# A two-layer encoder trunk: interleaved Strassen products, an earlier copy of the bias table, a gain moved from weights to x, and joined key and value weights

## The chip, the cores and the metric

The kernel runs on one core of a Trainium2 chip. The metric is the device time of one execution in microseconds (us). Five engines work beside each other: TensorE (PE, matrix products), VectorE (DVE), ScalarE (ACT), GpSimd (POOL) and SyncE (SP, which issues most of the DMAs). Each engine takes its instructions in the order in which the program lists them.

## The reference

Two layers work on x of 512 frames by 1024 features. Layer 0 is a gated linear recurrence with a squared-ReLU MLP, layer 1 a differential attention with another squared-ReLU MLP. Keys and values of layer 1 come from the stream after layer 0. All in fp32:

```python
h = h + rms_norm(hgrn2_mixer(rms_norm(h, a_norm_pre), a_w_in, ...), a_norm_post)
h = h + rms_norm(squared_relu_mlp(rms_norm(h, mlp_norm_pre[0]), w_up[0], w_down[0]), ...)
k, v = split(rms_norm(h, kv_norm) @ w_kv)          # 1024 x 2048
q = rms_norm(h, b_norm_pre) @ b_w_q                # 8 heads, two maps each
p = softmax(q k^T / 8 + rel_bias, block-causal); attn = p[0] - lam * p[1]
h = h + rms_norm(rms_norm(attn @ v, subln) * c @ b_w_out, b_norm_post)
h = h + rms_norm(squared_relu_mlp(..., w_up[1], w_down[1]), ...)   # relu(h W)^2 W'
```

## The kernel before

**Products.** Every fp32 operand of a large product is held as a pair: a rounded high part and the rest (`xhi`/`xlo`, `whi`/`wlo`, `uhi`/`ulo`), and a product is three matmuls on the fast fp32r type (`mm3`). Features lie on partitions, frames on the free axis. A weight tile of 128x1024 fp32 comes by a DMA of SP into one of four `raw` buffers; ACT writes the high part (`whi`), DVE the rest (`wlo`), each into a ring of eight tiles (`split_w`, L161 to 179). Where the norm's gain belongs to the weight's rows, a tile is split in pieces, one for each 128 rows, with the gain as scale (L175, L176); without a gain the whole tile goes in one instruction (L167, L168).

**Order.** The program is made by generators under a planner (`Plan`), which counts matmul time and puts the waits of the chains at due times (`yield 10.0` means "10 us of matmul time later"). It fixes PE's order. The other engines are ordered by a scheduler that follows the dependences; a chain's instructions get a higher priority than the main line's.

**Stages.** `first_loads` brings in x and the weights of head 0; `start` computes the first norm's factor, spreads it over the partitions as `dg` (L628), and a matmul `ps_sp` (L631) turns that into the row `rb`. `hgrn` runs the eight heads. Then come the output product, the MLP (`block`), the boundary with keys, queries and values of the first two heads (`attention_first`), `attention`, its output product, and the second MLP.

**MLP.** The hidden 4096 features are four quarters. Quarter 0 is a plain product (`up`). Quarters 1 to 3 use Strassen's seven products: a quarter has four pairs (of two column blocks), and a pair (`up_pair`, L452) makes seven products `prod` of 12 matmuls of 128x256, into three banks `ux`, `uy`, `uz`. The order in a pair is a11 (`ux`), s1 (`uz`), s2 (`ux`), a12 (`uy`), s3 (`ux`), s4 (`uz`), a22 (`ux`). `ux` goes on summing while ACT copies it out between: `p1` behind the first product, `u2` behind s2 (L486), `p5` from `uz`. After the last product ACT applies ReLU, square and split (L501 to 504, L409, L410). The next pair starts behind the last product. Each quarter ends with a down product (`dn`). I call the 28 products of a quarter a group: three groups in each layer.

**Bias table.** `params` spawns at 60 us of the MLP and waits `yield 40.0` (L648), makes a table `bw` of 16x640 on PE and DVE (L656 to 661), and POOL copies it 32 times over into `bias_dr` in DRAM (L662), which `attend` reads later.

**Attention.** In each group of two heads keys, queries and values come from three weights (`w_k`, `w_q`, `w_v`), in the order k, q, k, q, v; the values' weight is loaded after the other two. Units of 128 queries (`unit`) make logits, softmax, transposes `pt`, copies `at` on ACT (L902) and products `ao`.

Of the kernel before, what the change touches and what calls it, by code (L numbers as in the profile page):

```python
# [88 lines left out]
def trunk_kernel(ctx: ExitStack, tc: tile.TileContext, x_t, w_qf, w_g, w_i, w_ao, w_k, w_q, w_v, w_bo, w_up, w_us, w_dn,  # L89
# [301 lines left out]
    def block(pool, proj, gpost, name, layer, want):  # L391
# [60 lines left out]
        def up_pair(q, p, ts):  # L452

            nm = f"{layer}_{q}_{p}"
            def raw(n):
                return wp.tile([P, 2, 512], F32, tag="raw", name=f"raw_{n}{nm}", bufs=4)

            ws = w_us[layer, q - 1]
            ra = raw("a")
            nc.sync.dma_start(ra, ws[p, :, 0:3:2, :])  # L460

            rs = raw("s")
            for i in range(2):
                nc.sync.dma_start(rs[:, i, :], ws[p, :, 3, :])
            g.dma_start(rs, ws[p, :, 0:2, :], accum_op=ALU.add)  # L465
            if p % 2 == 0:
                rd = raw("d")
                nc.sync.dma_start(rd, ws[p:p + 2, :, 1, :].rearrange("a p f -> p a f"))
                a22s[:] = split_b(rd, f"d{nm}")
            a11, a12 = split_b(ra, f"a{nm}")  # L470
            a22 = a22s[p % 2]
            s3, s1 = split_b(rs, f"s{nm}")
            v.tensor_tensor(ra[:, 0, :], ra[:, 0, :], rs[:, 1, :], op=ALU.add)
            v.tensor_tensor(ra[:, 1, :], ra[:, 1, :], ra[:, 0, :], op=ALU.add)
            s2, s4 = split_b(ra, f"t{nm}")
            px, py, pz = mmt(f"ux{nm}")[:, 0:256], smt(f"uy{nm}")[:, 0:256], smt(f"uz{nm}")[:, 0:256]
            r = pool.tile([P, 2, S], F32, tag="r", name=f"r{nm}", bufs=2)

            def prod(ps, w, b, first):
# [9 lines left out]
            yield from prod(px, a11, xpart(0, 0), True)
            p1 = keep(px, "p1")  # L490
            yield from prod(pz, s1, ts[0], True)
            p5 = keep(pz, "p5")
            yield from prod(px, s2, ts[2], False)
            u2 = keep(px, "u2")
            yield from prod(py, a12, xpart(1, 0), True)
            v.tensor_tensor(r[:, 0, 0:256], py, p1, op=ALU.add)
            yield from prod(px, s3, ts[1], False)
            v.tensor_tensor(r[:, 1, 256:512], px, p5, op=ALU.add)
            yield from prod(pz, s4, xpart(1, 1), False)
            v.tensor_tensor(r[:, 0, 256:512], pz, u2, op=ALU.add)  # L500
            a.activation(r[:, 0, :], r[:, 0, :], AF.Relu)  # L501
            a.activation(r[:, 1, 256:512], r[:, 1, 256:512], AF.Relu, scale=-1.0)
            yield from prod(px, a22, ts[3], False)
            a.activation(r[:, 1, 0:256], px, AF.Relu, scale=-1.0)
            keep_u(r, p, 0, S)

        for q in range(4):
            if q == 0:
                wt = [load_w(w_up[layer, i], 512, None, f"up{layer}_{i}") for i in range(2)]
                for h, (lo, hi) in enumerate(halves):  # L510
                    yield until(("x", name, h))
                    for pr in range(4):
                        ps = mmt(f"up{layer}_{h}_{pr}").rearrange("p (j t) -> p j t", j=2)
                        for j in range(2):
                            n = 2 * pr + j
                            for kt in range(8):
                                wmm(ps[:, j, :], wt[n // 4], kt, (n % 4) * P, xhi, xlo, lo, hi, kt == 0, kt == 7)
                                yield 0
                        split_u(ps, pr, lo, hi, f"r{layer}_{h}_{pr}")
                ts = sums_x()  # L520
            else:
                for p in range(4):
                    yield from up_pair(q, p, ts)
# [52 lines left out]
    def first_loads(hp):  # L576
# [22 lines left out]
        for pr in range(4):  # L599
            for j in range(2) if pr == 0 else (slice(0, 2),):  # L600
                a.activation(xhi[pr][:, j], raws[pr][:, j], AF.Copy)  # L601
                v.tensor_tensor(xlo[pr][:, j], raws[pr][:, j], xhi[pr][:, j].bitcast(F32), op=ALU.subtract)  # L602
            if pr % 2 == 0:
                w0 += split_w(ws[pr // 2], gain, pr // 2, "qf0")
            sq.append(hp.tile([P, 2, S], F32, tag="vt", name=f"sqx{pr}", bufs=2) if pr < 2 else raws[pr])
            a.activation(sq[pr], raws[pr], AF.Square)
# [28 lines left out]
    def params(hp):  # L635
# [12 lines left out]
        yield 40.0  # L648
# [16 lines left out]
    def hgrn(hp, w0):  # L665
        apre = gn[:, G_APRE:G_APRE + 8]

# [106 lines left out]
        for p in range(4):  # L774
            for h in (2 * p, 2 * p + 1):
                if h >= 2:
                    yield until(("rec", h - 2))
                wt = w0 if h == 0 else load_w(w_qf[h], 256, apre, f"qf{h}")
# [16 lines left out]
            wv = load_w(w_i[p], 256, apre, f"wi{p}")  # L795
# [5 lines left out]
            wt = load_w(w_g[p], 256, apre, f"wg{p}")  # L801
# [38 lines left out]
    def attention(ap, f):  # L840
# [92 lines left out]
        for hq in range(4):  # L933
# [82 lines left out]
def _layout(i):  # L1016
# [21 lines left out]
    for n, s in enumerate(LEVELS):  # L1038
# [44 lines left out]
```

## Time and profile before

| | us |
|---|---|
| median of 3 runs | 1294.88 (1292.84 to 1295.48) |
| profiled execution | 1293.45 |
| its span in the trace | 1291.6 |
| PE busy in the span | 1256.5 |

Times in the trace count from the span's start. PE is busy for 97% of the span, so 35.1 us of it are idle on PE; "busy" counts a matmul from its start to its modelled end, also when it runs at a lower clock. The first quarter-group of layer 0 runs from 404 to 455 us, the boundary with keys and values from about 650 to 715, the attention from about 700 to 870, and the groups of layer 1 begin at about 1019, 1105 and 1192.

### The profile page before, as it was taken

How to read it: one execution, taken by the hardware profiler on the slowest of the kernel's cores; microseconds unless marked ns; L12 is line 12 of the kernel's file. 1: busy time of each engine (PE TensorE's matmuls, PEld its weight loads, DVE VectorE, ACT ScalarE, POOL GpSimd, SP SyncE). 2: the span in 40 equal slices, each digit the busy share in tenths (PEclk: the TensorE clock that was granted, in tenths of full speed). 3: DMA queues.
4: the chain of work that ended last, by engine and by line, in shares of the span. 5: the costliest groups of instructions: out<-in, count | busy, mean ns of one | idle time of the engine just before them, and what ended most of it. 6: DMA issues, size and time to landing. Idle time of an engine off the chain costs nothing.

```text
span 1291.6 us, 21535 instructions
## 1 busy us (share of the span) xinstructions
PE 1256.5 (97%) x8450; PEld 1139.7 (88%) x8450; DVE 824.1 (64%) x1731; ACT 665.2 (52%) x1321; POOL 78.4 (6%) x149
## 2 busy tenths in 40 slices
PE   8999999999997999999998999999999999999996
PEld 7989898999986989989998887889998898988996
DVE  7987777647853554636487978764785463663635
ACT  7553535247732634616454887674773371551732
POOL 0210101010000000000100000001000000000010
PEclk9999999999999999999998999999999999999998
DMA  6322222134355374544614432323336355463521
GB/s 242 110 82 66 66 66 82 50 101 154 108 147 96 101 203 99 172 104 115 212 51 154 139 107 70 103 69 95 129 110 160 94 171 120 115 180 81 167 79 66
DMA packets 53415, 149.89 MB, mean 116 GB/s; under 512 B 6049, under 2 KB 8354, under 8 KB 53314
## 3 DMA queue, kind: packets, MB, share of 16 engines
q1 hardware_dynamic: 44864, 119.82, 29.4%
q0 software_dynamic: 8208, 28.58, 10.1%
q8 instruction: 66, 1.08, 0.3%
q14 instruction: 35, 0.29, 0.1%
q10 hardware_dynamic: 242, 0.13, 0.0%
HBM read 138.80 MB, written 9.70 MB: 115 GB/s over the span
## 4 chain that ended last, share of the span: by engine, by line
PE 53%; ACT 5%; DVE 5%; DMA 4%; issue 1%; DVEq 0%; ACTq 0%; POOLq 0%; SPq 0%
PE dn L114 17%; PE kq L114 6%; PE dn_h L114 5%; PE ux L114 5%; PE up L114 4%; PE v L114 3%; PE bo_h L114 3%; DMA raw_s<-in_w_us_dram 3%; PE uz L114 2%; PE lg L114 2%; PE ao L114 1%; PE uy L114 1%; DVE wlo_s L447 1%; PE pt L119 1%; ACT r L409 1%
## 5 line engine op out<-in xcount | busy, mean ns | idle before, releaser
L114 PE MATMUL dn<-uhi,whi_dn 128*128 128x512 f32 x384 | 152.0, 396 | 0.0
L114 PE MATMUL dn<-ulo,whi_dn 128*128 128x512 f32 x384 | 151.9, 396 | 0.0
L114 PE MATMUL dn<-uhi,wlo_dn 128*128 128x512 f32 x384 | 151.9, 395 | 0.0
L168 DVE TENSOR_TENSOR wlo_dn<-raw_dn,whi_dn 128x1024 fp32r<-128x1024 f32 x64 | 77.5, 1221 | 17.9 <-ACT whi_dn L167 16.8
L446 ACT ACTIVATE whi_a<-raw_a 128x1024 fp32r<-128x1024 f32 x24 | 25.4, 1058 | 122.7 <-PE dn L114 114.1
L114 PEld LDWEIGHTS dn<-uhi,wlo_dn 128*128 128x128 f32 x384 | 72.2, 188 | 17.4
L114 PEld LDWEIGHTS dn<-uhi,whi_dn 128*128 128x128 f32 x384 | 72.2, 188 | 17.3 <-issue 0.2
L114 PEld LDWEIGHTS dn<-ulo,whi_dn 128*128 128x128 f32 x384 | 72.2, 188 | 17.1
L167 ACT ACTIVATE whi_dn<-raw_dn 128x1024 fp32r<-128x1024 f32 x64 | 67.1, 1055 | 17.9 <-PE ux L114 5.5
L114 PE MATMUL up<-xhi,whi_up 128*128 128x256 f32 x256 | 72.7, 284 | 0.0
L114 PE MATMUL up<-xlo,whi_up 128*128 128x256 f32 x256 | 71.9, 281 | 0.0
L114 PE MATMUL up<-xhi,wlo_up 128*128 128x256 f32 x256 | 71.9, 281 | 0.0
L411 DVE TENSOR_TENSOR ulo<-r,uhi 128x1024 fp32r<-128x1024 f32 (+1 forms) x40 | 40.2, 1009 | 47.0 <-ACT uhi L410 47.0
L114 PE MATMUL dn_h<-uhi,whi_dn 128*128 128x256 f32 x240 | 67.8, 282 | 0.0
L114 PE MATMUL dn_h<-ulo,whi_dn 128*128 128x256 f32 x240 | 67.4, 281 | 0.0
L114 PE MATMUL dn_h<-uhi,wlo_dn 128*128 128x256 f32 x240 | 67.4, 281 | 0.0
L540 DVE TENSOR_TENSOR zacc<-dn,zacc 128x512 f32<-128x512 f32 x32 | 22.1, 690 | 57.9 <-PE dn L114 57.8
L114 PE MATMUL qf<-xhi,whi_qf 128*128 128x512 f32 x128 | 53.1, 415 | 1.2 <-ACT xhi L601 0.9
L114 PE MATMUL qf<-xlo,whi_qf 128*128 128x512 f32 x128 | 50.8, 397 | 1.0 <-DVE xlo L602 1.0
L465 POOL DMA_DIRECT2D raw_s<-in_w_us_dram x24 | 20.8, 866 | 494.3 <-DMA raw_s<-in_w_us_dram 334.7
L114 PE MATMUL qf<-xhi,wlo_qf 128*128 128x512 f32 x128 | 50.6, 395 | 0.0
L114 PEld LDWEIGHTS up<-xlo,whi_up 128*128 128x128 f32 x256 | 48.2, 188 | 0.1
(373 smaller groups left out, 4102.3 us busy)
## 6 DMA issues: line engine op xcount, KB each, us to landing
raw_dn<-in_w_dn_dram SPq DMA_DIRECT2D x64, 512.0 KB, 4.4
raw_a<-in_w_us_dram SPq DMA_DIRECT2D x24, 512.0 KB, 4.3
raw_s<-in_w_us_dram SPq DMA_DIRECT2D x48, 256.0 KB, 4.5
raw_s<-in_w_us_dram POOLq DMA_DIRECT2D x24, 512.0 KB, 6.5
raw_up<-in_w_up_dram SPq DMA_DIRECT2D x16, 512.0 KB, 3.9
raw_qf<-in_w_qf_dram SPq DMA_DIRECT2D x15, 512.0 KB, 3.9
raw_d<-in_w_us_dram SPq DMA_DIRECT2D x12, 512.0 KB, 4.4
raw_wi<-in_w_i_dram SPq DMA_DIRECT2D x8, 512.0 KB, 3.8
```

Source lines behind the costliest of these rows:

```text
L114: nc.tensor.matmul(out, lhsT, rhs, **kw)
L119: nc.tensor.transpose(out, in_, identity)
L167: a.activation(hi, raw, AF.Copy)
L168: v.tensor_tensor(lo, raw, hi.bitcast(F32), op=ALU.subtract)
L409: a.activation(r, r, AF.Square)
L411: v.tensor_tensor(ulo[pr][:, :, lo:hi], r, uhi[pr][:, :, lo:hi].bitcast(F32), op=ALU.subtract)
L446: a.activation(hi, raw, AF.Copy)
L447: v.tensor_tensor(lo, raw, hi.bitcast(F32), op=ALU.subtract)
L465: g.dma_start(rs, ws[p, :, 0:2, :], accum_op=ALU.add)
L540: v.tensor_tensor(z, pss[n4], z, op=ALU.add)
```

## The change

Four parts. (1) A pair becomes a class with a beginning (a11, s1), a middle and an end (a22). `up_pairs` issues the next pair's beginning ahead of the end of this one; and in the first three pairs of a group s3 stands behind s4 (in the last one, `alone`, ahead of it as before). (2) `params` waits 15 instead of 40 us. (3) In the recurrence the pre-norm gain is put in x when it is split (`gain` as scale, in halves of 128x512), and the weights are split without a gain, whole tiles at a time; head 0's first tile is split in two halves. (4) `w_k` and `w_v` become one weight `w_kv` with tiles of 512 columns (256 of keys, 256 of values), loaded with `w_q` ahead of it (`load_qkv`); queries are multiplied before keys (the last two lines of the diff; 0 and 1 stand for keys, 2 and 3 for queries). The loads, splits and banks in the class `Pair` are those of `up_pair`.

```diff
-        def up_pair(q, p, ts):
+        class Pair:
...
+            def begin(self):
+                yield from self.prod(self.x, self.a11, xpart(0, 0), True)
+                self.p1 = self.keep(self.x, "p1")
+                yield from self.prod(self.z, self.s1, self.t1, True)
+                self.p5 = self.keep(self.z, "p5")
+            def go_on(self, alone):
+                yield from self.prod(self.x, self.s2, self.t2, False)
+                u2 = self.keep(self.x, "u2")
+                yield from self.prod(self.y, self.a12, xpart(1, 0), True)
+                v.tensor_tensor(self.r[:, 0, 0:256], self.y, self.p1, op=ALU.add)
+                if alone:
+                    yield from self.seventh()
+                yield from self.prod(self.z, self.s4, xpart(1, 1), False)
+                v.tensor_tensor(self.r[:, 0, 256:512], self.z, u2, op=ALU.add)
+                a.activation(self.r[:, 0, :], self.r[:, 0, :], AF.Relu)
+                if not alone:
+                    yield from self.seventh()
+            def seventh(self):
+                c22 = self.r[:, 1, 256:512]
+                yield from self.prod(self.x, self.s3, self.t3, False)
+                v.tensor_tensor(c22, self.x, self.p5, op=ALU.add)
+                a.activation(c22, c22, AF.Relu, scale=-1.0)
+            def end(self):
+                yield from self.prod(self.x, self.a22, self.t4, False)
+                a.activation(self.r[:, 1, 0:256], self.x, AF.Relu, scale=-1.0)
+                keep_u(self.r, self.p, 0, S)
+        def up_pairs(q, ts):
+            one = Pair(q, 0, ts)
+            yield from one.begin()
+            for p in range(1, 5):
+                yield from one.go_on(p == 4)
+                if p < 4:
+                    other = Pair(q, p, ts)
+                    yield from other.begin()
+                yield from one.end()
+                one = other
...
-                a.activation(xhi[pr][:, j], raws[pr][:, j], AF.Copy)
-                v.tensor_tensor(xlo[pr][:, j], raws[pr][:, j], xhi[pr][:, j].bitcast(F32), op=ALU.subtract)
+                a.activation(xhi[pr][:, j], raws[pr][:, j], AF.Copy, scale=gc)
+                v.scalar_tensor_tensor(xlo[pr][:, j], raws[pr][:, j], gc, xhi[pr][:, j].bitcast(F32),
+                                       op0=ALU.mult, op1=ALU.subtract)
...
-        yield 40.0
+        yield 15.0
...
-                wt = w0 if h == 0 else load_w(w_qf[h], 256, apre, f"qf{h}")
+                wt = w0 if h == 0 else load_w(w_qf[h], 256, None, f"qf{h}")
...
+    def load_qkv(hq):
+        wq = load_w(w_q[hq], 256, gn[:, G_BPRE:G_BPRE + 8], f"wq{hq}")
+        wkv = load_w(w_kv[hq], 512, gn[:, G_KV:G_KV + 8], f"wkv{hq}")
+        return wq, [tuple(w[:, 0:256] for w in kt) for kt in wkv], [tuple(w[:, 256:512] for w in kt) for kt in wkv]
...
-            for i in range(4):
+            for i in (2, 3, 0, 1):
...
-            for i in (0, 2, 1, 3):
+            for i in (2, 0, 3, 1):
```

The next rows are ACT's instructions before, in layer 1's first group, at the passage from pair 0 (`r1_1_0`) to pair 1 (`p11_1_1`, `p51_1_1`, `u21_1_1` are its copies out of the banks; `whi_t1_1_2` a weight of pair 2).

```order
L502 ACTIVATE r1_1_0_10525<-r1_1_0_10525 128x256
L501 ACTIVATE r1_1_0_10525<-r1_1_0_10525 128x512
L504 ACTIVATE r1_1_0_10525<-ux1_1_0_10522 128x256
L409 ACTIVATE r1_1_0_10525<-r1_1_0_10525 128x1024
L486 ACTIVATE p11_1_1_10661<-ux1_1_1_10645 128x256
L410 ACTIVATE uhi0_74<-r1_1_0_10525 128x1024
L446 ACTIVATE whi_t1_1_2_10770<-raw_a1_1_2_10748 128x1024
L486 ACTIVATE p51_1_1_10675<-uz1_1_1_10647 128x256
L486 ACTIVATE u21_1_1_10689<-ux1_1_1_10645 128x256
```

The same place in the changed kernel.

```order
L507 ACTIVATE r1_1_0_10279<-r1_1_0_10279 128x512
L515 ACTIVATE r1_1_0_10279<-r1_1_0_10279 128x256
L489 ACTIVATE p11_1_1_10399<-ux1_1_1_10383 128x256
L446 ACTIVATE whi_t1_1_2_10508<-raw_a1_1_2_10486 128x1024
L489 ACTIVATE p51_1_1_10413<-uz1_1_1_10385 128x256
L519 ACTIVATE r1_1_0_10279<-ux1_1_0_10276 128x256
L409 ACTIVATE r1_1_0_10279<-r1_1_0_10279 128x1024
L410 ACTIVATE uhi0_74<-r1_1_0_10279 128x1024
L489 ACTIVATE u21_1_1_10443<-ux1_1_1_10383 128x256
```

Both copies of pair 1 now stand ahead of the last ReLU, the square and the split of pair 0 (`ux1_1_0` to `uhi0`), which come behind them in one run; `u21_1_1` is still behind that run.

The next rows are DVE's instructions before, ahead of the square matrix `dg` that the matmul `ps_sp` reads, in the first 30 us (`nt`, `rcol` are steps of the norm's factor, `wlo_wi0`, `wlo_wg0`, `wlo_qf2` weights that are used later).

```order
L214 SCALAR_TENSOR_TENSOR nt_278<-rcol_93 128x4
L176 SCALAR_TENSOR_TENSOR wlo_wi0_1_380<-raw_wi0_1_377,gn_82,whi_wi0_1_379 128x256
L215 TENSOR_TENSOR nt_278<-nt_278,nx_277 128x4
L176 SCALAR_TENSOR_TENSOR wlo_wi0_1_380<-raw_wi0_1_377,gn_82,whi_wi0_1_379 128x256
L216 SCALAR_TENSOR_TENSOR rcol_93<-nt_278,rcol_93 128x4
L176 SCALAR_TENSOR_TENSOR wlo_wg0_0_534<-raw_wg0_0_531,gn_82,whi_wg0_0_533 128x256
L628 TENSOR_TENSOR dg_290<-ident_84,rcol_93 128x512
```

The same place in the changed kernel.

```order
L168 TENSOR_TENSOR wlo_qf2_0_684<-raw_qf2_0_681,whi_qf2_0_683 128x1024
L214 SCALAR_TENSOR_TENSOR nt_264<-rcol_93 128x4
L215 TENSOR_TENSOR nt_264<-nt_264,nx_263 128x4
L216 SCALAR_TENSOR_TENSOR rcol_93<-nt_264,rcol_93 128x4
L168 TENSOR_TENSOR wlo_qf2_1_690<-raw_qf2_1_687,whi_qf2_1_689 128x1024
L659 TENSOR_TENSOR dg_276<-ident_84,rcol_93 128x512
```

Pieces of 256 columns between the steps have become whole tiles, and two tiles of head 2's weight (`wlo_qf2_0`, `wlo_qf2_1`), which before came behind `dg`, now stand ahead of it.

The last rows are POOL's DMAs around the copy of the bias table before (`raw_s0_1_0` to `raw_s0_1_3` are the loads of the four pairs of layer 0's first group, `res_ao1` is the stream stored at the boundary ahead).

```order
L465 DMA raw_s0_1_0_4084<-in_w_us_dram 128x1024
L465 DMA raw_s0_1_1_4213<-in_w_us_dram 128x1024
L465 DMA raw_s0_1_2_4336<-in_w_us_dram 128x1024
L662 DMA bias_dr_103<-tb_4044 512x1x640
L465 DMA raw_s0_1_3_4465<-in_w_us_dram 128x1024
```

The same place in the changed kernel.

```order
L468 DMA raw_s0_1_0_3902<-in_w_us_dram 128x1024
L468 DMA raw_s0_1_1_4015<-in_w_us_dram 128x1024
L693 DMA bias_dr_103<-tb_3711 512x1x640
L468 DMA raw_s0_1_2_4138<-in_w_us_dram 128x1024
L468 DMA raw_s0_1_3_4267<-in_w_us_dram 128x1024
```

The copy is one load earlier on POOL, ahead of the third pair's accumulating load; PE's small products for the table have moved from the second half of the down product ahead of this group into its first half.

## Rows read from the trace of the kernel before

**Rows 1.** Engine totals on the page: busy us, share of the span, instructions.

```profile
PE 1256.5 (97%) x8450; PEld 1139.7 (88%) x8450; DVE 824.1 (64%) x1731; ACT 665.2 (52%) x1321; POOL 78.4 (6%) x149
```

**Rows 2.** Waits of PE, whole span: who waited, for whom, total us, times, longest.

```profile
PE ux L114 <- ACT u L486: 7.9, 6, 6.6
PE v L114 <- DVE wlo_wv L176: 5.3, 2, 3.7
PE ux L114 <- ACT p L486: 3.8, 7, 0.8
...
PE gl L114 <- DVE sc L700: 0.5, 1, 0.5
```

**Rows 3.** Table by windows: busy us (instructions) of each engine, granted clock, DMA share, GB/s.

```profile
400.00:455.00 55.00, 47.17 (x356) 45.53 (x355) 29.33 (x36) 28.93 (x43) 0.86 (x1) 0.94 0.55 122
```

**Rows 4.** PE in time, first group of products: start, length, instruction, idle before, releaser.

```profile
403.98 0.28 PE L114 MATMUL ux<-xhi,whi_a 128*128 128x256 f32 x1
...
405.40 0.40 PE L114 MATMUL uz<-t,whi_s 128*128 128x256 f32 x2
...
416.40 0.80 PE L114 MATMUL ux<-t,whi_s 128*128 128x256 f32 x2 [6.55 <-ACT u L486]
...
419.13 0.41 PE L114 MATMUL uz<-xhi,whi_t 128*128 128x256 f32 x1
```

**Rows 5.** One tile's matmuls by form, same group: count, ns min/median/max, first and last start.

```profile
L114 PE MATMUL ux<-xhi,whi_d x16: 277/282/323, 421.2 to 454.3; 128*128 128x256 f32 x16
```

**Rows 6.** ACT in time, same stretch.

```profile
415.02 1.06 ACT L446 ACTIVATE whi_d<-raw_d 128x1024 fp32r<-128x1024 f32 x1 [7.61 <-DMA raw_d<-in_w_us_dram]
```

**Rows 7.** POOL in time, same stretch.

```profile
398.65 0.68 POOL L662 DMA_DIRECT2D bias_dr<-tb  x1 [10.58 <-DVE tb L661]
```

**Rows 8.** DMA view, 385 to 420: issuing queue, KB each, median us to landing.

```profile
bias_dr<-tb POOLq DMA_DIRECT2D x1, 1280.0 KB, 15.0
...
raw_d<-in_w_us_dram SPq DMA_DIRECT2D x1, 512.0 KB, 11.0
```

**Rows 9.** DMA issues on the page, whole span, the same load.

```profile
raw_d<-in_w_us_dram SPq DMA_DIRECT2D x12, 512.0 KB, 4.4
```

**Rows 10.** ACT in time, fourth group, second pair.

```profile
1041.08 1.06 ACT L409 ACTIVATE r<-r 128x1024 f32<-128x1024 f32 x1
...
1042.04 0.37 ACT L486 ACTIVATE p<-ux 128x256 f32<-128x256 f32 x1
```

**Rows 11.** PE in time, same stretch.

```profile
1042.46 0.51 PE L114 MATMUL ux<-t,whi_t 128*128 128x256 f32 x2 [0.50 <-ACT p L486]
...
1044.00 0.28 PE L114 MATMUL uy<-xhi,whi_a 128*128 128x256 f32 x1
```

**Rows 12.** PE in time, values product at the boundary after the first MLP.

```profile
687.11 0.28 PE L114 MATMUL v<-whi_wv,xhi 128*128 128x256 f32 x1
...
693.19 0.38 PE L114 MATMUL v<-wlo_wv,xhi 128*128 128x256 f32 x1 [3.70 <-DVE wlo_wv L176]
...
695.39 0.58 PE L114 MATMUL v<-wlo_wv,xhi 128*128 128x256 f32 x1 [1.58 <-DVE wlo_wv L176]
...
700.87 0.28 PE L114 MATMUL kq<-xhi,whi_wk 128*128 128x256 f32 x1
```

**Rows 13.** DVE in time, same boundary, last quarter of the new x.

```profile
695.65 0.68 DVE L336 TENSOR_TENSOR xlo<-rs_m,xhi 128x512 fp32r<-128x512 f32 x1
```

**Rows 14.** DVE in time, first norm's square, with a run of pieces.

```profile
28.33 0.68 DVE L628 TENSOR_TENSOR dg<-ident,rcol 128x512 f32<-128x512 f32 x1
28.93 2.46 DVE L176 SCALAR_TENSOR_TENSOR wlo_wg<-raw_wg,gn,whi_wg 128x256 fp32r<-128x256 f32 x6
```

**Rows 15.** PE in time, the matmul that reads it.

```profile
30.07 1.02 PE L114 MATMUL ps_sp<-dg,ones 128*128 128x512 f32 x2
```

**Rows 16.** ACT in time, end of the second values product in the attention.

```profile
770.67 1.71 ACT L175 ACTIVATE whi_wk<-raw_wk,gn 128x256 fp32r<-128x256 f32 x4 [0.46 <-PE v L114]
...
772.64 0.96 ACT L902 ACTIVATE at<-pt 128x384 f32<-128x384 f32 x2
```

More of the change, by code (lines that the diff above doesn't have):

```diff
@@ L88, in trunk_kernel @@
 @with_exitstack
-def trunk_kernel(ctx: ExitStack, tc: tile.TileContext, x_t, w_qf, w_g, w_i, w_ao, w_k, w_q, w_v, w_bo, w_up, w_us, w_dn,
+def trunk_kernel(ctx: ExitStack, tc: tile.TileContext, x_t, w_qf, w_g, w_i, w_ao, w_kv, w_q, w_bo, w_up, w_us, w_dn,
                  gains, lam_p, rel, onehot, ident_d, mask_d, out_t):
@@ L450, in block @@
         a22s = []
-        def up_pair(q, p, ts):
[L454 to L479, printed above, removed]
@@ new lines, in block, with __init__, raw, prod @@
+        class Pair:
+            def __init__(self, q, p, ts):
+                self.p, self.nm, ws = p, f"{layer}_{q}_{p}", w_us[layer, q - 1]
+                self.t1, self.t3, self.t2, self.t4 = ts
+                def raw(n):
+                    return wp.tile([P, 2, 512], F32, tag="raw", name=f"raw_{n}{self.nm}", bufs=4)
+                ra = raw("a")
+                nc.sync.dma_start(ra, ws[p, :, 0:3:2, :])
+                rs = raw("s")
+                for i in range(2):
+                    nc.sync.dma_start(rs[:, i, :], ws[p, :, 3, :])
+                g.dma_start(rs, ws[p, :, 0:2, :], accum_op=ALU.add)
+                if p % 2 == 0:
+                    rd = raw("d")
+                    nc.sync.dma_start(rd, ws[p:p + 2, :, 1, :].rearrange("a p f -> p a f"))
+                    a22s[:] = split_b(rd, f"d{self.nm}")
+                self.a11, self.a12 = split_b(ra, f"a{self.nm}")
+                self.a22 = a22s[p % 2]
+                self.s3, self.s1 = split_b(rs, f"s{self.nm}")
+                v.tensor_tensor(ra[:, 0, :], ra[:, 0, :], rs[:, 1, :], op=ALU.add)
+                v.tensor_tensor(ra[:, 1, :], ra[:, 1, :], ra[:, 0, :], op=ALU.add)
+                self.s2, self.s4 = split_b(ra, f"t{self.nm}")
+                self.x, self.y, self.z = [t(f"u{n}{self.nm}")[:, 0:256] for t, n in ((mmt, "x"), (smt, "y"), (smt, "z"))]
+                self.r = pool.tile([P, 2, S], F32, tag="r", name=f"r{self.nm}", bufs=2)
+            def prod(self, ps, w, b, first):
@@ L482, in prod, with keep @@
                     yield 0
-            def keep(ps, name):
-                t = pool.tile([P, 256], F32, tag="ev", name=f"{name}{nm}", bufs=4)
+            def keep(self, ps, name):
+                t = pool.tile([P, 256], F32, tag="ev", name=f"{name}{self.nm}", bufs=4)
                 a.activation(t, ps, AF.Copy)
                 return t
[L489 to L505, printed above, removed]
+            def begin(self):
[3 more added lines that the diff above has]
+                self.p5 = self.keep(self.z, "p5")
@@ L521, in block @@
             else:
-                for p in range(4):
-                    yield from up_pair(q, p, ts)
+                yield from up_pairs(q, ts)
             if q < 3:
@@ L599, in first_loads @@
         for pr in range(4):
-            for j in range(2) if pr == 0 else (slice(0, 2),):
-                a.activation(xhi[pr][:, j], raws[pr][:, j], AF.Copy)
-                v.tensor_tensor(xlo[pr][:, j], raws[pr][:, j], xhi[pr][:, j].bitcast(F32), op=ALU.subtract)
-            if pr % 2 == 0:
-                w0 += split_w(ws[pr // 2], gain, pr // 2, "qf0")
+            for j in range(2):
+                gc = gain[:, 2 * pr + j:2 * pr + j + 1]
+                a.activation(xhi[pr][:, j], raws[pr][:, j], AF.Copy, scale=gc)
+                v.scalar_tensor_tensor(xlo[pr][:, j], raws[pr][:, j], gc, xhi[pr][:, j].bitcast(F32),
+                                       op0=ALU.mult, op1=ALU.subtract)
+                if pr == 0:
+                    w0 += split_w(ws[0][:, 2 * j:2 * j + 2, :], None, j, "qf0")
+            if pr == 1:
+                w0 += split_w(ws[1], None, 2, "qf0")
+        for pr in range(4):
             sq.append(hp.tile([P, 2, S], F32, tag="vt", name=f"sqx{pr}", bufs=2) if pr < 2 else raws[pr])
@@ L800, in hgrn @@
                 keep_values(vt, ps, t2)
-            wt = load_w(w_g[p], 256, apre, f"wg{p}")
+            wt = load_w(w_g[p], 256, None, f"wg{p}")
             for j in range(2):
```

23 lines of the change are left out of this document (8 added, 15 removed).

## The prediction

> **What bounds the kernel now.** I read the engine totals first: PE is busy for 1256.5 of 1291.6 us [rows 1]. No part of the change takes a matmul away, so all that it can gain lies in the 35.1 us in which PE is idle, and in matmuls that run slowly behind an idle time. The reader is to see next, in the waits of PE, for whom it is idle: 7.9 us for the copies `u2`, 3.8 for `p1`, 5.3 for the values' weight [rows 2]. The recurrence's worst wait there is 0.5 us: it has next to nothing to give, and much to lose. Third I read those places in time.
>
> The first group of products is the costly one. Twelve matmuls take 1.42 us (403.98 to 405.40), but between the fourth product and `ux` at 416.40 PE waits 6.55, and the next twelve take 2.73, to 419.13 [rows 4]. The granted clock of this window is 0.94 [rows 3]; a pace of about half is that of the lower level, 1.2 against 2.4 GHz, and it is seen right behind this wait. From the first start to the last `whi_d` start there are 50.3 us [rows 4, 5]; 27 products of 1.42 and nine matmuls of 0.118 more would take 39.4, so the group loses 10.9. What ends last before 416.40 is `u2`; it is queued on ACT behind the split `whi_d`, which began at 415.02, 7.61 us late for its load [rows 6]. That load took 11.0 us, the same load 4.4 over the span [rows 8, 9]. Beside it runs the bias copy of 1280 KB, issued on POOL at 398.65 and 15.0 us under way [rows 7, 8], so until 413.7.
>
> In the other five groups PE's waits are short: 3.0 for `p1` (3.8 less one of 0.8 in the first group) and 1.35 for `u2` (7.9 less 6.55), 11 in number [rows 2]. For instance `p1` began at 1042.04, behind the square of the pair before, which began at 1041.08 and takes 1.06 [rows 10]. A wait costs more than its idle time: twelve matmuls from 1042.46 take 1.54 instead of 1.42, and a shown length of 0.28 against a pace of 0.12 hides another 0.16 [rows 4, 11]; 0.28 together. So the five groups lose 4.35 + 11 x 0.28 = 7.4.
>
> At the boundary the values product (48 matmuls) runs from 687.11 to 700.87, 13.76 us, with waits of 3.70 and 1.58 for `wlo_wv` and a slow stretch behind them [rows 12]; at 0.118 each it would take 5.7, so 8.1 are lost.
>
> **Part 2, the bias copy.** `yield 15.0` puts the table's products about 25 us of matmul time earlier, so the copy starts at about 374 to 377 (398.65 less 25; it stands behind the second pair's load on POOL) and, at 15.0, ends at 392 at the latest. The late load is still issued only when its buffer is free, at about 404 (415.02 less 11.0), but then alone: 4.4 us, 408.4, split 1.06, `u2` at about 409.8. With part 1's order s3 is the sixth product and not the fifth, wanted at 403.98 + 5 x 1.42 = 411.1. So this wait goes with its slow stretch: of 10.9, 1.75 are two later waits (`p1` 0.8 and a split, with 0.28 each) and belong to part 1. The copy's new neighbours are the third pair's loads, whose products start 13 x 1.42 = 18 us into the group, at 422; even 7 us late they hold up nobody. About 0.6 may stay at the last pair (next part), so I take -10.3 for the whole group, range -9 to -10.9.
>
> A rule that speaks against this: the copy took 15.0 us [rows 8]. The Trainium skill (SBUF — State Buffer, "The DMA setup-cost knee (why "@ 1 MiB" ≠ asymptote)") fits a transfer as 2 us plus its bytes over 436 GB/s, by which an estimate for 1.31 MB is 5.0 us; then the copy would have been over at 403.7 before the late load was issued, and its move would give nothing. The trace differs, and it decides; by the fit the sum would be 9 smaller, which is rival 3.
>
> **Part 1, the products.** `p1` of the next pair now stands ahead of the last ReLU, square and split of this one (first pair of order excerpts), and `ux` of the pair before gets one product (1.42) in between, more than the longest wait of 0.8. `u2` has two products instead of one before s3 reads on. Only the last pair keeps the old order behind a run of ReLU, square and split (0.4 + 2 x 1.0) that starts when a22 ends: `u2` is ready about 3.0 us after that, wanted at 2 x 1.42 = 2.84, so 0.2 to 0.5 a group may stay. 5 x 0.2 = 1.0: I take -6.3 of 7.4, range -3.3 to -7.4.
>
> **Part 4, the boundary.** Queries' and joint weights are loaded one after the other and all split before the second half of x comes through DVE, so neither wait for `wlo_wv` returns; the product ends 8.1 earlier, at 692.8. What is late next is x itself: the second pass reads the last quarter's rest at its 20th matmul, 692.8 + 19 x 0.118 = 695.0, and `xlo` was ready at 695.65 + 0.68 = 696.3 [rows 13]. Unchanged it costs 1.3 + 0.28; if the loads ahead of it on ACT land 0.7 earlier, as buffers come free sooner, 0.6 + 0.28; if the joint splits push it 0.8 back, 2.4. I take -7.0, range -5.5 to -8.1.
>
> It has a price in the attention. Joint tiles stay in use until the last values matmul, and the pieces queued on ACT there are twice as wide. Now four pieces of 256 take 1.71 ahead of `at` [rows 16], 0.43 each; whole tiles of 1024 take 1.06 [rows 6]; 512 lies between, 0.57 by width. Four such are 0.6 more, at two of the three places; at the third three whole tiles of the output weight stand ahead of `at`, 3.0 instead of 1.7. PE already waits there, so it is paid: 0.6 + 0.6 + 1.3 = +2.5, bounds 0 (unlike order of arrival) and 5.1 (all double).
>
> **Part 3, the gain.** A tile's split is one instruction of 1.06 instead of four in 1.71 on ACT [rows 6, 16], and on DVE one instead of four at 2.46/6 = 0.41 [rows 14]. Both engines have room, so this gains nothing on PE. But the order shows two whole tiles of head 2 ahead of `dg`, which wait for their loads. `dg` ran from 28.33 to 29.01, `ps_sp` at 30.07, so 1.06 is spare [rows 14, 15]. Bounds: 0 if the loads come early; 3.3 if two tiles waiting one for the other and two more stand in line (4 x 1.1 - 1.06). The loads come when raw buffers are freed, some microseconds earlier than now; I put `dg` at 30.5: +1.3. First products of x: halves arrive 1 us earlier, and an add moved ahead of the third `xlo` takes it back: 0, between -1.2 and +0.5. Elsewhere in the recurrence 0 to +1; I take +0.5.
>
> **Sum.** -10.3 - 6.3 - 7.0 + 2.5 + 1.3 + 0.5 = -19.3. Against the profiled execution, 1293.45, that is 1274.2; the median stands 1.4 above it, so 1275.6, and I say 1275.5. Adding the ends that go together, this case reaches from about 1271 to 1280.
>
> **Rivals.**
> 1. *The boundary's wait only moves.* The keys' product comes to the last joint tile before it is split, or x's chain, whose steps stand between the pieces on ACT and DVE, is pushed back by 4 us or more. For: now the last piece is ready only after 693, with far smaller tiles, and a slow stretch came right behind such waits [rows 12]. Against: the new order has nothing of x's chain between the last two tiles. Of 7.0, 0 to 3 are left: 1280 to 1282.
> 2. *ACT remains the limit in the groups.* The run of three moves to `u2` and to the next pair's `p1`. For: all five groups wait on ACT alone [rows 2]. Against: 1.42 more room than the worst wait of 0.8. Gain 0 to 3 instead of 6.3: 1279 to 1282.
> 3. *The copy does not hold the load.* If its bytes are through before the load is issued, and only its end is reported late, the load is slow for a reason of its own; 9 to 10 of the 10.3 stay, about 1285. For: the copy has a lead of 5 us. Against: copy and load end within 1.3 us of each other, 413.7 and 415.0 [rows 6 to 8]. The fit in the Trainium skill, named above, would make it so.
> 4. *Slower: whole tiles block the recurrence.* 32 tiles (16 of `qf`, 8 of `wi`, 8 of `wg`) on two engines in order are 64 blocks, each longer by 1.06 - 0.43 = 0.63 for whatever stands behind it. If PE waits for all, +40; it outweighs 19.3 from 31 of 64 on, and at three quarters gives 30 - 19 = +11: 1306. For: heads are chains of small steps through DVE, ACT and PE. Against: PE's waits in the recurrence are 0.5 at most, so the chains have room, and the engines' total work falls.
>
> **How the numbers follow.** My forecast 0.58, rival 1 0.13, rival 2 0.11, rival 3 0.07, rival 4 0.05, and 0.06 for two of the first three together or other small losses (1283 to 1290). A measurement of this kernel can tell 0.2%, 2.6 us, from no change. All but rival 4 are faster by more; from it and the rest I put 0.04 on slower, 0.03 on same, 0.93 on faster. The range reaches from 1270.5 to 1284.5: it leaves out rival 4, most of rival 3 and some of the mixed cases.
>
> **What would show it.** Right: in the first group no wait over 1 us, the load near 4.4 and the bias copy landed before 400; `ux` waits for `p1` gone in all groups; `v` without waits for its weight, and a wait of `kq` for `xlo` under 1.5; `ps_sp` waiting for `dg` by 1 to 2; `ao` waiting for `at` by about 1 and up to 2. Wrong: `ux` waiting for `u` in every pair, a long wait of `kq` for a joint weight, a stretch with granted clock well under 1 in the boundary, or waits over 1 us in the recurrence.

## The result and the profile after

| | us |
|---|---|
| median after | 1281.06 (1280.87 to 1282.29) |
| median before, same chip | 1294.85 |
| ratio after to before | 0.9898, 95% interval 0.9881 to 0.9915 |
| profiled execution after, its span | 1280.94, 1279.2 |

The change gains 13.8 us by the medians and 12.4 by the spans of the two profiled executions. The forecast was 1275.5: the time lies in the range, but 5.6 above the likeliest value.

First the engine totals on the page after [rows 1], then PE's waits over the span [rows 2].

```profile
PE 1254.5 (98%) x8450; PEld 1135.7 (89%) x8450; DVE 807.2 (63%) x1607; ACT 642.5 (50%) x1197; POOL 80.4 (6%) x149
```

```profile
PE dn_h L114 <- ACT r L519: 2.1, 2, 1.6
PE ps_sp L114 <- DVE dg L659: 2.0, 1, 2.0
PE ux L114 <- DVE r L514: 1.7, 4, 0.6
...
PE ao L114 <- ACT at L935: 1.2, 3, 0.6
...
PE lg L114 <- DVE mx L919: 0.5, 1, 0.5
```

PE's own work is the same, its idle time falls from 35.1 to 24.7 us. The three waits that headed the list before (`u`, `wlo_wv`, `p`; 17.0 us together) are all gone. Three new ones have come: `dn_h`, `ps_sp` and `ux` for DVE, 5.8 us together. The question of the experiments is what these three are and what they cost.

**First group.** First the window of 400 to 455 us [rows 3], then the group's first and last `ux` forms [rows 4, 5].

```profile
400.00:455.00 55.00, 54.36 (x398) 51.16 (x397) 35.36 (x42) 35.26 (x50) 1.73 (x2) 1.00 0.55 155
```

```profile
L114 PE MATMUL ux<-xhi,whi_a x16: 277/280/283, 407.8 to 438.2; 128*128 128x256 f32 x16
...
L114 PE MATMUL ux<-xhi,whi_d x16: 277/280/386, 419.2 to 448.5; 128*128 128x256 f32 x16
```

From 407.8 to 448.5 are 40.7 us, where it was 50.3; the granted clock is 1.00, where it was 0.94. The cause, which the experiment only_copy below confirms, stands in the DMA view of 376 to 412 us and on ACT [rows 8, 6].

```profile
bias_dr<-tb POOLq DMA_DIRECT2D x1, 1280.0 KB, 17.1
...
raw_a<-in_w_us_dram SPq DMA_DIRECT2D x2, 512.0 KB, 10.2
raw_s<-in_w_us_dram SPq DMA_DIRECT2D x2, 256.0 KB, 11.3
raw_d<-in_w_us_dram SPq DMA_DIRECT2D x1, 512.0 KB, 3.7
```

```profile
411.57 1.06 ACT L446 ACTIVATE whi_d<-raw_d 128x1024 fp32r<-128x1024 f32 x1 [0.30 <-DMA raw_d<-in_w_us_dram]
412.53 0.36 ACT L489 ACTIVATE u<-ux 128x256 f32<-128x256 f32 x1
```

The load of `raw_d` takes 3.7 instead of 11.0 us, and ACT waits 0.30 for it, not 7.61. The copy is as slow as before, but it now slows `raw_a` and `raw_s`, for which PE does not wait.

**Boundary.** PE in time, to be read against [rows 12].

```profile
681.24 0.28 PE L114 MATMUL v<-whi_wkv,xhi 128*128 128x256 f32 x1
...
686.83 0.28 PE L114 MATMUL kq<-xhi,whi_wq 128*128 128x256 f32 x1
...
689.41 0.38 PE L114 MATMUL kq<-xhi,whi_wq 128*128 128x256 f32 x1 [0.29 <-ACT xhi L335]
...
690.15 0.39 PE L114 MATMUL kq<-xlo,whi_wq 128*128 128x256 f32 x1 [0.35 <-DVE xlo L336]
```

The values product takes 5.59 us instead of 13.76, and what is late next is x: two short waits, 0.64 together.

**Start.** DVE and then PE in time around the first norm's `dg` [rows 14, 15], and the window of 30 to 40 us, before and then after (the granted clock is the third number from the end).

```profile
29.14 1.23 DVE L168 TENSOR_TENSOR wlo_qf<-raw_qf,whi_qf 128x1024 fp32r<-128x1024 f32 x1 [0.78 <-ACT whi_qf L167]
...
30.94 1.23 DVE L168 TENSOR_TENSOR wlo_qf<-raw_qf,whi_qf 128x1024 fp32r<-128x1024 f32 x1
32.08 0.69 DVE L659 TENSOR_TENSOR dg<-ident,rcol 128x512 f32<-128x512 f32 x1
```

```profile
21.77 1.95 PE L114 MATMUL ps_mc<-onesd,sqx 128*128 128x1 f32 x16 [0.33 <-DVE sqx L639]
...
32.82 1.99 PE L114 MATMUL ps_sp<-dg,ones 128*128 128x512 f32 x2 [2.02 <-DVE dg L659]
33.82 1.42 PE L114 MATMUL qf<-xhi,whi_qf 128*128 128x512 f32 x1
```

```profile
30.00:40.00 10.00, 10.00 (x69) 8.94 (x69) 8.69 (x17) 9.09 (x19) 3.08 (x6) 1.00 0.45 153
```

```profile
30.00:40.00 10.00, 7.99 (x34) 5.73 (x33) 7.31 (x13) 6.04 (x8) 0.37 (x1) 0.83 0.68 235
```

`dg` stands behind two whole tiles of head 2 and starts at 32.08, where it was 28.33. PE waits 2.02, and then the two matmuls of `ps_sp` take 1.99 instead of 1.02: the granted clock of the window is 0.83, where it was 1.00, a mean that holds a stretch at the lower level of 1.2 GHz. PE comes to `ps_sp` 2.75 later than before and to the first product of `wi` 4.5 later: 0.7 come ahead of the wait (0.33 of them at `ps_mc`, for the sum of squares `sqx`), 2.0 are the wait, 1.8 come behind it.

**Passage between pairs.** ACT, DVE and PE in time, first group.

```profile
427.23 1.06 ACT L446 ACTIVATE whi_s<-raw_s 128x1024 fp32r<-128x1024 f32 x1 [2.57 <-DMA raw_s<-in_w_us_dram]
```

```profile
428.33 1.23 DVE L447 TENSOR_TENSOR wlo_s<-raw_s,whi_s 128x1024 fp32r<-128x1024 f32 x1 [1.83 <-ACT whi_s L446]
429.47 0.42 DVE L514 TENSOR_TENSOR r<-ux,p 128x256 f32<-128x256 f32 x1
```

```profile
429.94 0.39 PE L114 MATMUL ux<-xhi,whi_d 128*128 128x256 f32 x1 [0.56 <-DVE r L514]
```

`c22` of pair 1 (L514) is a sum that had its inputs; it stands on DVE behind the rest of pair 3's `s`, whose load landed late. a22 goes on summing in the bank that this sum reads, so PE waits.

**Down product behind a group.** ACT and PE in time, last group of layer 0.

```profile
621.80 1.06 ACT L167 ACTIVATE whi_dn<-raw_dn 128x1024 fp32r<-128x1024 f32 x1 [1.05 <-DMA raw_dn<-in_w_dn_dram]
...
623.29 0.36 ACT L519 ACTIVATE r<-ux 128x256 f32<-128x256 f32 x1
```

```profile
623.70 0.39 PE L114 MATMUL dn_h<-uhi,whi_dn 128*128 128x256 f32 x1 [1.64 <-ACT r L519]
```

The last ReLU of the group stands on ACT behind a split that waits for its load; `dn_h` waits for this ReLU, which frees the bank `ux` of the last pair.

### The profile page after: what moved, and what is told of

It is laid out like the page before. It is cut to its first block, busy times and chain, and to the rows that moved or that the text cites. A ratio compares the mean times of both kernels' runs of the same rounds, so it can differ in the third digit from the quotient of the medians.

```text
span 1279.2 us, 21323 instructions
## 1 busy us (share of the span) xinstructions
PE 1254.5 (98%) x8450; PEld 1135.7 (89%) x8450; DVE 807.2 (63%) x1607; ACT 642.5 (50%) x1197; POOL 80.4 (6%) x149
## 3 DMA queue, kind: packets, MB, share of 16 engines
q0 software_dynamic: 8208, 28.58, 10.2%
## 4 chain that ended last, share of the span: by engine, by line
PE 82%; DMA 7%; DVE 5%; ACT 4%; issue 2%; SPq 0%; DVEq 0%; ACTq 0%; POOLq 0%
PE dn L114 20%; PE up L114 7%; PE dn_h L114 6%; PE kq L114 6%; PE ux L114 6%; PE qf L114 6%; PE g L114 4%; DMA raw_s<-in_w_us_dram 4%; PE i L114 4%; PE bo_h L114 3%; PE ao_h L114 3%; PE gl L114 3%; PE v L114 3%; PE uz L114 2%; PE lg L114 2%
## 5 line engine op out<-in xcount | busy, mean ns | idle before, releaser
L167 ACT ACTIVATE whi_dn<-raw_dn 128x1024 fp32r<-128x1024 f32 x64 | 66.4, 1053 | 12.4 <-PE ux L114 4.2
L446 ACT ACTIVATE whi_t<-raw_a 128x1024 fp32r<-128x1024 f32 x24 | 25.5, 1061 | 49.4 <-PE dn L114 27.2
```

The costliest lines, as they stand in the source:

```text
L167: a.activation(hi, raw, AF.Copy)
L446: a.activation(hi, raw, AF.Copy)
```

## The experiments

All stand against the kernel before on the same chip, with the 95% interval of the ratio. The next table takes the profiled executions stage by stage: how much later (+) or earlier a stage's first matmul comes than before, less the shift at the stage's own start. "Start" goes to the first product of `wi` (about 38 us), "rest" to the first group; the five other groups go together; "`dn_h` 0" is the down product behind layer 0's last group, and the attention goes to the first product of the second MLP; "tail" is what comes behind the last group.

| | start | rest | first group | five groups | `dn_h` 0 | boundary | attention | tail | span |
|---|---|---|---|---|---|---|---|---|---|
| after | +4.5 | -0.7 | -9.6 | -4.0 | +1.9 | -7.0 | +1.8 | +0.8 | -12.4 |
| only_products | -0.7 | -0.2 | -1.1 | -5.4 | 0.0 | -0.5 | 0.0 | +1.2 | -6.7 |
| only_copy | 0.0 | -0.2 | -8.5 | -0.5 | 0.0 | -0.6 | 0.0 | +0.1 | -9.7 |
| only_gain | +2.6 | -0.7 | -0.2 | +1.6 | 0.0 | -0.4 | 0.0 | 0.0 | +3.0 |
| only_kv | -0.1 | -0.2 | +0.3 | -0.7 | 0.0 | -6.4 | +1.8 | +0.1 | -5.2 |
| dg_ahead | +2.2 | -0.5 | -10.2 | -3.6 | +4.3 | -6.7 | +1.8 | +1.6 | -11.2 |
| pieces | +0.1 | 0.0 | -10.1 | -5.7 | +2.2 | -7.0 | +1.8 | +1.0 | -17.6 |
| sum_ahead | +2.5 | -0.7 | -10.5 | -6.6 | +0.7 | -6.8 | +1.8 | 0.0 | -19.6 |
| kv_apart | +4.7 | -0.7 | -10.2 | -5.6 | 0.0 | -7.0 | -0.1 | +1.0 | -18.1 |
| squares_ahead | +0.1 | -0.7 | -9.9 | -4.4 | +2.3 | -7.0 | +1.8 | +1.1 | -16.9 |
| all_mended | +1.3 | 0.0 | -10.5 | -6.6 | 0.0 | -7.1 | -0.1 | +0.1 | -22.7 |
| mended_without_gain | +0.7 | 0.0 | -10.5 | -6.6 | 0.0 | -7.2 | -0.1 | +0.1 | -23.7 |

Stages that an edit does not touch differ by up to 2.4 us from kernel to kernel (start of sum_ahead, `dn_h` 0 of dg_ahead and kv_apart), so a single entry under that is read only together with the wait behind it. A profiled execution is also not the median: that of dg_ahead lies 3.5 us above its median, those of only_products, kv_apart and squares_ahead 1.7 to 2.0 below theirs.

**One part at a time**, four kernels made from the one before. The cut shows a line or two of each; the other lines of the same part go with them.

```diff
# only_products: part 1
-                for p in range(4):
-                    yield from up_pair(q, p, ts)
+                yield from up_pairs(q, ts)
# only_copy: part 2
-        yield 40.0
+        yield 15.0
# only_gain: part 3
+                wt = w0 if h == 0 else load_w(w_qf[h], 256, None, f"qf{h}")
# only_kv: part 4
+        wkv = load_w(w_kv[hq], 512, gn[:, G_KV:G_KV + 8], f"wkv{hq}")
```

> The kernel before with part 1 alone (interleaved products), everything else as before. Theory: the late load of the first group stays, but s3 is the sixth product there, so that wait falls from 6.55 to about 5.1 us with its slow stretch behind it: first group -1.4, its two later waits 1.75 less one new wait of 0.84; the other five groups gain 4.0 and give 2.6 back at the two down products that read by halves (dn_h waiting for ACT's last ReLU, 1.6 and 0.5 us, plus refill). Sum about -3.7 us, 1291. Rival (interleaving gains its full 7.4 in the groups and the waits of dn_h come from another part): -8 to -9. Rival (the groups gain only because the copy was moved): 0.

> The kernel before with part 2 alone (the bias copy about 25 us of matmul time earlier). Theory: the bias copy holds up the load; the wait of 6.55 us and its slow stretch go, the two waits of 0.8 and 0.4 stay: -8.8 us, 1286. Rival (the copy does not hold the load): 0, 1295, with the load still 11 us on its way.

> The kernel before with part 3 alone (gain in x, whole tiles split in the recurrence). Theory: dg comes about 3 us late behind whole tiles of head 2, ps_sp waits about 2 us, and matmuls behind it run at half pace for some 2 us: +3.8, 1298.7. Rival (the late dg comes from the parts together or from chance): within 1 us of 0.

> The kernel before with part 4 alone (joint key and value weights, queries first). Theory: the boundary gives 7.0, the attention takes 1.8 back (1.4 in three later ao, the rest at a logit): -5.2, 1289.7. Rival (the attention's loss belongs to another part): -7, 1288. Rival (x's chain moves without the other parts): -3 or less.

Measured: only_products 0.9969 (0.9955 to 0.9984), only_copy 0.9931 (0.9914 to 0.9947), only_gain 1.0021 (1.0011 to 1.0031), only_kv 0.9969 (0.9956 to 0.9982). Of 1293.24 that is -4.0, -8.9, +2.7 and -4.0, together -14.2, beside -13.2 for 0.9898: the medians of the parts add up within their intervals. The profiled executions add up less well: -18.6 against -12.4. The start (+1.8 against +4.5) and `dn_h` 0 (0.0 against +1.9) hold 4.6 of these 6.2, so a share of the shortfall shows only where the parts stand together. First the wait that part 1 alone leaves in the first group, then the load that part 2 alone sets free (DMA view of 365 to 420 us).

```profile
415.52 0.79 PE L114 MATMUL ux<-t,whi_s 128*128 128x256 f32 x2 [5.12 <-ACT u L489]
```

```profile
bias_dr<-tb POOLq DMA_DIRECT2D x1, 1280.0 KB, 17.2
raw_a<-in_w_us_dram SPq DMA_DIRECT2D x2, 512.0 KB, 10.1
...
raw_d<-in_w_us_dram SPq DMA_DIRECT2D x1, 512.0 KB, 3.6
```

With the copy where it was, PE still waits 5.12 for `u2`; with the copy alone moved, the first group gets 8.5 of its 9.6. Part 3 costs time on its own: in only_gain the wait of `ps_sp` is 0.78, and yet the start loses 2.6. There the slow stretch stands in the window of 20 to 30 us, behind a wait of 0.34 at `ps_mc`:

```profile
20.00:30.00 10.00, 9.66 (x44) 7.81 (x43) 8.25 (x17) 3.84 (x5) 0.00 (x0) 0.83 0.74 240
```

**dg_ahead**: the rests of head 2's tiles on DVE behind `dg` (an order without a wait of its own).

```diff
             rest = v.tensor_tensor(lo, raw, hi.bitcast(F32), op=ALU.subtract)
+            if name == "qf2":
+                behind(rest, first["dg"])
```

> The changed kernel with one thing more: the rests of head 2's two weight tiles are kept behind dg in DVE's order. Theory A (the order makes dg late, and the wait behind it brings the half pace): dg ready by about 30, ps_sp without a wait, no slow stretch: -3.9 us, 1277. Theory B (the half pace comes from the start, where x now arrives in another rhythm, as with part 3 alone where it stood at 23 to 26 us): the wait goes, the slow stretch stays or moves: -2.2. Rival (something else sets dg): 0, ps_sp still at 32.5.

Measured 0.9880 (0.9860 to 0.9899), 2.3 us better than after, with intervals that overlap. The wait of `ps_sp` is gone, but the start still loses 2.2. The rows are PE in time, and the window of 20 to 30 us.

```profile
21.73 1.95 PE L114 MATMUL ps_mc<-onesd,sqx 128*128 128x1 f32 x16 [0.34 <-DVE sqx L647]
23.54 0.47 PE L114 MATMUL qf<-xhi,whi_qf 128*128 128x512 f32 x1
```

```profile
20.00:30.00 10.00, 9.66 (x43) 7.74 (x43) 8.82 (x19) 3.98 (x4) 0.00 (x0) 0.83 0.65 220
```

The clock's 0.83 now stands in this window and no longer in 30 to 40: there is a slow stretch behind the wait of 0.34 for the sum of squares. `after` has that short wait too, with its slow stretch only later, at `ps_sp`. So dg_ahead does not show what the order of `dg` costs: in only_gain and sum_ahead, which leave that order as it is, the slow stretch stands behind `ps_mc` as well, and their starts lose 2.6 and 2.5, hardly more than the 2.2 here. The rows are `dg` in dg_ahead, only_gain and sum_ahead.

```profile
28.92 0.69 DVE L667 TENSOR_TENSOR dg<-ident,rcol 128x512 f32<-128x512 f32 x1
```

```profile
31.79 0.68 DVE L633 TENSOR_TENSOR dg<-ident,rcol 128x512 f32<-128x512 f32 x1
```

```profile
31.70 0.69 DVE L667 TENSOR_TENSOR dg<-ident,rcol 128x512 f32<-128x512 f32 x1
```

Where PE has lost its time before, it comes so late to `ps_sp` that a late `dg` costs only 0.78 and 0.24 of wait. The +4.3 at `dn_h` 0 are a wait of 2.7 with another slow stretch (granted clock 0.83 from 615 to 625 us).

**squares_ahead**: dg_ahead, and the rest of head 1's second tile behind the last sum of squares.

```diff
+            if name == "qf1" and pr == 1:
+                behind(rest, first["sq"])
```

> The kernel dg_ahead with the rest of head 1's second tile kept behind the last sum of squares on DVE, so that ps_mc finds it ready. Theory (the wait of 0.34 at ps_mc brings the half pace between 23 and 26 us): wait and slow stretch go, -1.7 to -2 us against dg_ahead. Rival (the half pace comes from the first 15 us, whatever ps_mc finds): the stretch stays at 23 or moves, 0.

```profile
20.00:30.00 10.00, 10.00 (x52) 8.17 (x50) 8.44 (x18) 3.64 (x4) 0.00 (x0) 1.00 0.65 205
```

Measured 0.9864 (0.9846 to 0.9883). The short wait is gone, the clock stays at 1.00, and the start loses 0.1: with both orders mended, whole tiles cost the start nothing. In the table that is 2.1 better than dg_ahead; the medians differ by 0.0016 of 1294.85, 2.1 us, with intervals that overlap.

**pieces**: part 3 kept, but the tiles of the start split per 128 rows, as before.

```diff
+        if gain is None and name in ("qf1", "wi0", "wg0", "qf2", "qf3"):
+            for j in range(per):
+                a.activation(hi[:, j, :], raw[:, j, :], AF.Copy)
+                v.tensor_tensor(lo[:, j, :], raw[:, j, :], hi[:, j, :].bitcast(F32), op=ALU.subtract)
```

> The changed kernel, but the weights of heads 1 to 3, of the first values and of the first gate are split in pieces of 256 columns as before (still without a gain). If the whole tiles between the steps of the norm's factor are the cause, dg is back at 28 to 30 and the gain is that of keeping dg ahead, -2 to -3.9 us; if the gain in x itself costs the time, 0.

Measured 0.9866 (0.9846 to 0.9886). Both waits are gone (`dg` begins at 27.66), the start loses 0.1. So the gain in x costs the start nothing. The loss comes from what stands on DVE ahead of the sum of squares and of `dg`: narrow pieces mend it, and so do whole tiles in the order of squares_ahead.

**sum_ahead**: on DVE the rest and the sums of pair p's `s` behind the sum `c22` of pair p-2; on ACT the last down tile's split behind the last ReLU.

```diff
-                self.s3, self.s1 = split_b(rs, f"s{self.nm}")
-                v.tensor_tensor(ra[:, 0, :], ra[:, 0, :], rs[:, 1, :], op=ALU.add)
+                self.s3, self.s1 = split_b(rs, f"s{self.nm}", c22s.get(p - 2))
+                behind(v.tensor_tensor(ra[:, 0, :], ra[:, 0, :], rs[:, 1, :], op=ALU.add), c22s.get(p - 2))
...
+                wt = [load_w(w_dn[layer, q, i], 512, None, f"dn{layer}_{q}_{i}", c21[0] if i else None) for i in range(2)]
```

> The changed kernel with the rest of pair 3's s tile (and the sum that reads its load) kept behind DVE's sum r of pair 1, and the split of the last down tile kept behind ACT's last ReLU of the group. Theory: the four waits of ux for DVE r (0.6 each at most, 1.7 in all, 2.8 with what follows) and the two of dn_h for ACT r (2.1, with refill 2.6) go: -5.4, 1275.7. Rival (they only change place: the next thing in the queue is as late): less than 2 us gained, with new waits for p, u or whi_s.

Measured 0.9843 (0.9826 to 0.9859), 7.1 us better than after. PE's waits now:

```profile
PE qf L114 <- DVE xlo L637: 1.3, 3, 0.8
PE ao L114 <- ACT at L943: 1.2, 3, 0.6
...
PE dn_h L114 <- ACT r L526: 0.5, 1, 0.5
```

`ux` waits for nothing any more, and `dn_h` 0.5 instead of 2.1. The groups give -6.6 and -10.5; with `dn_h` and the tail these four stages are 5.5 better than after, which is what the edit is worth by these entries. Another 2.0 lie at the start, which it does not touch: here the slow stretch stands behind `ps_mc`, and `ps_sp` waits 0.24.

```profile
20.00:30.00 10.00, 9.66 (x44) 7.78 (x43) 8.39 (x16) 4.40 (x5) 0.00 (x0) 0.83 0.73 228
```

**kv_apart**: from the second group of heads on, keys and values come from the joint weight as two tiles of 256 columns, the values' behind the keys'.

```diff
+        if hq > 0:
+            return wq, load_w(w_kv[hq][:, :, 0:256], 256, gn[:, G_KV:G_KV + 8], f"wk{hq}"), None
```

> The changed kernel with joint key and value tiles for the first two heads alone; for the other six keys and values are loaded and split apart again in 256 columns, values after keys, from the same array in DRAM. Theory: the three waits of ao at the end of a values product shrink to their old size: -1.2 us, and -0.5 more if the wait of a logit for DVE goes too. Rival (the loads from an array with longer rows, 1 KB out of 2, are slower and give waits for weights): 0 or slower.

Measured 0.9870 (0.9850 to 0.9889), 3.6 us better than after, with intervals that just overlap; 1.9 lie in the attention, the rest in stages that this edit does not touch. ACT at the end of the values product, in `after` and then in kv_apart, against [rows 16].

```profile
757.85 2.55 ACT L175 ACTIVATE whi_wkv<-raw_wkv,gn 128x512 fp32r<-128x512 f32 x4
760.31 0.96 ACT L935 ACTIVATE at<-pt 128x384 f32<-128x384 f32 x2
```

```profile
755.01 1.71 ACT L175 ACTIVATE whi_wq<-raw_wq,gn 128x256 fp32r<-128x256 f32 x4 [0.46 <-PE v L114]
...
756.98 0.96 ACT L937 ACTIVATE at<-pt 128x384 f32<-128x384 f32 x2
```

Four pieces ahead of `at` take 2.55 in `after` and 1.71 here, as before the change, and the attention's loss goes from +1.8 to -0.1. The boundary's gain stays.

**all_mended** is pieces, sum_ahead and kv_apart together; **mended_without_gain** is the change without part 3, with sum_ahead and kv_apart.

```diff
# mended_without_gain, against all_mended
-                a.activation(xhi[pr][:, j], raws[pr][:, j], AF.Copy, scale=gc)
+                a.activation(xhi[pr][:, j], raws[pr][:, j], AF.Copy)
```

> The changed kernel with three things mended: early weights of the recurrence in pieces, DVE's and ACT's sums kept ahead as in sum_ahead, and key and value tiles apart after the first two heads. Theory (the three places are independent): -3.7 in the first 40 us, -4.5 to -5.5 in the groups and the down products, -1.9 in the attention, together about -10: 1270.5 to 1271.5. Rival (they share slack, the next wait is as late): above 1274.

> The same without part 3: weights of the recurrence carry the gain in pieces as before the change, x does not. If part 3 is worth nothing where ACT and DVE have room: the same time as all_mended within 1 us. Rival (fewer instructions on ACT and DVE help somewhere in the recurrence): 1 us or more slower than all_mended.

Measured 1270.65 us, 0.9808 (0.9789 to 0.9826), and 1269.74 us, 0.9801 (0.9783 to 0.9818). Both beat the kernel before and the changed one (0.9898), with intervals that stand apart from it. The two can't be told from each other: no gain of part 3 shows here. A wait at the start that is new in all_mended, and then one that has grown in mended_without_gain:

```profile
PE i L114 <- DVE k L713: 0.9, 1, 0.9
```

```profile
PE qf L114 <- ACT xhi L635: 1.7, 2, 1.1
```

Each has a wait of about 1 us of its own there (`xhi` took 0.9 in all before), so neither start is free.

## Why the prediction was right in part

**Part 2, right.** -10.3 was forecast for the first group, -9.6 came. The copy started at 380.2, 3 to 6 us later than forecast, and ended at 397.3 instead of 392; the load was still issued behind it and took 3.7. Rival 3 (the copy does not hold the load) fell with only_copy: nothing but the copy's place changed, and 8.5 us came.

**Part 4, right at the boundary, in size alone in the attention.** The boundary was forecast at -7.0 and gave -7.0, by its own steps: the product 8.2 shorter, then 1.2 back for x (8.1 and 1.1); beside the forecast wait for `xlo` stands one for `xhi`. That the figure fits so closely is in part luck: only_kv alone gives -6.4, and kernels without part 4 have -0.4 to -0.6 there. Rival 1 did not come. The attention's price was +2.5 and measured +1.8. Four pieces of 512 cost 0.84 more than four of 256 (forecast 0.6), but little of it reached PE: `ao` waits for `at` 1.2 in all, where it was 1.0. About 0.8 of the 1.8 come at the first logits, where one waits 0.52 for DVE, a wait that the forecast did not have; kv_apart has neither the wait nor the loss.

**Part 1, the step that failed.** "So 0.2 to 0.5 a group may stay" was forecast, hence -6.3. The copies `p1` and `u2` did stop holding PE, as said; but the groups gave -4.0, and 2.7 went behind them (`dn_h` 1.9, tail 0.8). The step followed ACT's run of ReLU, square and split and asked for no other reader of the banks. There were two: the sum `c22` on DVE, and the last ReLU, which must free a bank for the down product. Both had been put behind a split that waits for a load. sum_ahead shows it: with both ahead, the five groups give -6.6, the size that the step had named. How much such a place costs hangs on when its load lands: only_products lost 0.0 at `dn_h` 0 without that order. Rival 2 had the right size (a gain of 0 to 3, measured 1.3) by a wrong way, since ACT's run was not the limit.

**Part 3, the other step that failed.** `dg` was put at 30.5 and began at 32.08: two whole tiles stood between the steps of the norm, 1.1 each, and the first was 0.78 late itself. So 2.0 of wait came and not 1.3. The larger miss is the 1.8 behind it, at the lower clock, which the prediction had priced in the first group and forgot here; 0.7 more came ahead of the wait, where it had put 0: +4.5 instead of +1.3. Rival 4 (whole tiles hold up the recurrence everywhere) was wrong in size: the rest of the recurrence is 0.7 faster, all the loss is in the first 38 us.

Sum of the measured stages: 4.5 - 0.7 - 9.6 - 4.0 + 1.9 - 7.0 + 1.8 + 0.8 = -12.3, the span's -12.4 up to rounding, against a forecast of -19.3. Of the 7 between them the start has 3.2, the groups and what follows them 5.0, the first group 0.7; the rest of the recurrence (1.2) and the attention (0.7) give back. That the time lies in the range is in part luck. For its own case the prediction gave 1271 to 1280, and 1281.06 is outside that. It lies where the range had room for rivals 1 and 2, and neither came as described. Two terms missed their own bounds, part 1 (-1.3 with what followed, against -3.3 to -7.4) and part 3 at the start (+4.5, against at most 3.8: 3.3 for `dg` and 0.5 for the first products of x).

**Open.** Five of the thirteen kernels have a wait of 0.33 to 0.34 at `ps_mc`, and each of them has one slow stretch in its first 40 us: right behind `ps_mc` in only_gain, dg_ahead and sum_ahead, at `ps_sp` in `after` and kv_apart. The eight without this wait have none (granted clock 1.00 in both windows), not even all_mended with its wait of 0.9 at `i`. What decides between the two places was not settled. Why `dn_h` 0 waited 0 to 2.7 in kernels whose edits lie elsewhere was seen only as far as the load of `raw_dn` that lands before or after ACT's order wants it.

## What to carry to other kernels

When an order is changed to free one engine's copies, list every reader of the banks that the moved products write again, on every engine, and look at what stands ahead of it there: a ready sum behind a split whose load is late is a wait that no table of busy times shows. Such a place is mended by an order of two instructions alone, here worth 5.5 us in the stages concerned. A wait early in a stage is priced with the slow stretch behind it, and wider blocks on an engine are looked at where a short chain of small steps has to pass between them.

## What the runs showed of the hardware

A copy of 1280 KB from a tile of 16 partitions took 15.0, 17.1 and 17.2 us in three kernels, and in the changed kernel the loads of `raw_a` and `raw_s` beside it took 10.2 and 11.3, where the page of the profile has 4.3 and 4.2 over the span. The Trainium skill (SBUF — State Buffer, "The DMA setup-cost knee (why "@ 1 MiB" ≠ asymptote)") gives a fit by which an estimate for it is 5.0 us; the measurements are three times as long, and they decide. The same section of the Trainium skill names 436 GB/s as the limit of 16 ports and asks for transfers over 128 partitions, which this copy is not, so the difference does not speak against the fit where it applies. A slow stretch of the clock behind a wait of only 0.34 us had not been expected: it stands in only_gain, dg_ahead and sum_ahead (granted clock 0.83 from 20 to 30 us), whose starts lose 2.2 to 2.6, and squares_ahead, without the wait, lost 0.1. Right behind that wait PE ran 16 matmuls of one column (`ps_mc`).
